# A state-space mixer with its gate's product read from PSUM, its norm in six calls, and one product moved from GpSimd to ScalarE

## The chip, the cores and the metric

The kernel runs on one core of a Trainium2 chip. A core has five engines that run side by side, each through its own list of instructions in order: TensorE (PE, the matrix products; its weight loads are listed apart as PEld), VectorE (DVE), ScalarE (ACT), GpSimd (POOL) and SyncE (SP, here a queue of DMAs). They meet in semaphores only. The on-chip memory is SBUF; matrix products land in PSUM, of which there are eight banks. The metric is the device time of one execution in microseconds (us).

## The reference

A trunk of two layers over 1040 tokens (16 learned ones ahead of 1024) of 1024 features: layer 0 is a Mamba-2 state-space mixer (SSD) and a gated FFN with a convolution, layer 1 a stick-breaking attention and the same kind of FFN. The change is in the mixer alone:

```python
z, xbc, dt_raw = split(u @ w_in)                 # 2048 + 3072 + 32 columns
xbc = silu(causal_dwconv(xbc, conv_w, conv_b))   # 4 taps
xs, b_in, c_in = split(xbc)                      # 2048 | 4 groups x 128 | 4 x 128
dt = softplus(dt_raw + dt_bias); xdt = xs * dt
a_cs = cumsum(dt * -exp(a_log))                  # within a chunk
y_diag = (c_in . b_in) * exp(a_cs[l] - a_cs[s]) @ xdt       # s <= l
chunk_states = b_in^T @ (exp(a_cs[-1] - a_cs) * xdt)
y = y_diag + exp(a_cs) * c_in @ state + d_skip * xs
hg = y * silu(z)                                  # per group of 512 columns:
hg = hg * rsqrt(mean(hg * hg) + eps) * gate_g
out = hg @ w_out
```

## The kernel before

Features lie on partitions, tokens along the row. Each fp32 product is made of three of rounded parts (`mm3`, L150 to L155: high by high, high by low, low by high), so a projection of one block of 128 columns over one of three token tiles (348, 348 and 344 tokens, `TT`) is 24 matmuls into one PSUM bank `pj`. The mixer (from L637 on) first projects group 0's six blocks (four of `x`, one of `b`, one of `c`), and then runs a loop of four groups by nine chunks of 116 tokens. A chunk is `ssd_front`, some projection tiles, and `ssd_back`. The tiles come from one stream, numbered n here: the blocks into group 1, gate of group 0, into group 2, gate of 1, into 3, gate of 2, gate of 3; 18 tiles go by during group 0, 30 during each of groups 1 and 2, 18 during group 3 (two a chunk in groups 0 and 3, three or four in 1 and 2), 6 are left over. Inside this loop the lists of PE, DVE, ACT and POOL are in the order in which the code is written; SP's DMAs are put in order by a scheduler.

- A tile of an `into` block: 24 matmuls (PE), the convolution's first tap by ACT (L275) and three more by DVE (L278), a silu by ACT (L459) that is issued with the next tile.
- A tile of a gate block: 24 matmuls, silu from the bank into an SBUF buffer `z` by ACT (L491), product with the group's `y` rows in place by DVE (L498), square by ACT (L503), sum over the group's four blocks by DVE (L507, L509). In group 3 the product waits until its chunk is done.
- The norm of a gate group, one call for each token tile (`gate_norm`, L515): `rstd` sums the squares over partitions by a matmul into a bank `ms` (L186), takes Ln and Exp on ACT (L189, L190) with a table load ahead of them (L177), refines by four DVE operations (L191 to L194, the second of which reads `ms`), and then four DVE operations scale the rows (L520). The calls stand ahead of tiles n = 31, 32, 33 (61, 62, 63 and 91, 92, 93). Behind the third of groups 0 and 1 the rows are sent to DRAM by four POOL DMAs (`spill`, L357, `y_d`), and their SBUF buffers go to later `xbc` blocks.
- `ssd_front`: on PE c·b (`cb`), the four transposes `px` of x, and the transpose `pb` of b; on DVE the masked `cbm`, `xdt` = px · dt (L597), and the decay matrix times `cbm` (L598); on ACT the copy `bk` of `pb` (L604); on POOL `xde` = xdt · decay to the chunk's end (L606).
- `ssd_decays` of the next chunk is issued in three parts behind the tiles: DMA loads of D and E; eight DVE subtractions (L573) and an Exp on ACT (L574); E times c on POOL (L577).
- `ssd_back`: the state's matmul `S` = bk · xde (L619), the state's update (POOL L625, DVE L626), 16 matmuls `y` (L631, L633) and four DVE operations that add them to the rows (L635).

PSUM in this loop: the projection turns over three banks; `cb`, `pb`, `ms` and `y` over three (pool `sm`); `px` and `S` over two.

## Time and profile before

| | |
|---|---|
| median of the runs | 3048.41 us (3046.30 to 3048.53) |
| the profiled execution | 3046.06 us, its span 3044.3 |
| PE, PEld busy | 95%, 91% of the span |
| DVE, ACT, POOL busy | 76%, 54%, 43% |
| granted TensorE clock, mean | 0.979 |

The four-group loop runs from about 150 to about 740 us; everything ahead and behind keeps its order. Rows give engine, line, operation, out<-in without buffer numbers, partitions x elements; a line number is one of the kernel before unless said. In the timeline `[2.58 <-DVE z L192]` means that the engine stood idle for 2.58 us ahead of that instruction and what released it.

### The profile page before, as it was taken

Reading aid. Unit: us, or ns where it says so; the run is one execution under the profiler, and the core shown is the slowest. Engines: PE = TensorE matmul, PEld = TensorE weight load, DVE = VectorE, ACT = ScalarE, POOL = GpSimd, SP = SyncE. Lnnn points to the kernel's source line nnn. Section 1 sums busy time; section 2 is a strip of 40 time slices with the busy share of each in tenths; the row PEclk is TensorE's granted clock in tenths of the full one; section 3 lists DMA queues with packets and bytes.
Section 4 is the critical chain, followed back from the end, with each engine's and each line's share of the span. In section 5 each row is a group of like instructions: output and inputs, shape, how many; then the busy total and the mean of one; then the engine's idle time right before and its main releaser. Section 6 shows DMA issues by size and latency. Waiting matters only on the chain. (4 is left out here: it accounts for less than half of the span.)

```text
span 3044.3 us, 58681 instructions
## 1 busy us (share of the span) xinstructions
PE 2887.7 (95%) x22535; PEld 2771.6 (91%) x22535; DVE 2312.5 (76%) x4062; ACT 1650.1 (54%) x3403; POOL 1310.2 (43%) x1257
## 2 busy tenths in 40 slices
PE   5999999989997999999999999999898999999997
PEld 2999898979997999998999999999797999999996
DVE  3686868885459877888876888888759888778874
ACT  3555555553245565555334888887636555655332
POOL 1154434452225766663343222222335666663441
PEclk8999999999998999999999999999998999999998
DMA  3333333323121222225232222221431222225231
GB/s 115 106 94 91 109 89 104 103 75 135 61 93 56 75 80 84 77 88 186 64 127 80 59 65 64 68 61 50 141 106 64 84 78 74 81 85 189 77 99 56
DMA packets 123221, 273.42 MB, mean 90 GB/s; under 512 B 13468, under 2 KB 53020, under 8 KB 122940
## 3 DMA queue, kind: packets, MB, share of 16 engines
q1 hardware_dynamic: 117622, 258.54, 27.3%
q10 hardware_dynamic: 4054, 6.56, 0.6%
q8 instruction: 177, 2.90, 0.4%
q0 software_dynamic: 1264, 4.57, 0.4%
q14 instruction: 104, 0.85, 0.1%
HBM read 201.25 MB, written 53.45 MB: 84 GB/s over the span
## 5 line engine op out<-in xcount | busy, mean ns | idle before, releaser
L153 PE MATMUL pj<-uh,wh 128*128 128x348 f32 (+2 forms) x1536 | 506.3, 330 | 9.5 <-ACT bk L604 6.4
L154 PE MATMUL pj<-ul,wh 128*128 128x348 f32 (+2 forms) x1536 | 497.7, 324 | 0.0
L155 PE MATMUL pj<-uh,wl 128*128 128x348 f32 (+2 forms) x1536 | 495.7, 323 | 0.7 <-POOL wl L1150 0.7
L154 PE MATMUL p<-bl,fh 128*128 128x262 f32 x1408 | 401.2, 285 | 14.0 <-DVE bl L814 14.0
L153 PE MATMUL p<-bh,fh 128*128 128x262 f32 x1408 | 402.1, 286 | 1.6 <-ACT fh L845 1.1
L155 PE MATMUL p<-bh,fl 128*128 128x262 f32 x1408 | 400.2, 285 | 0.0
L846 POOL TENSOR_TENSOR fl<-x,fh 128x1024 fp32r<-128x1024 f32 x88 | 212.5, 2415 | 363.2 <-ACT fh L845 277.4
L147 POOL TENSOR_TENSOR wl<-w,wh 128x1024 fp32r<-128x1024 f32 (+2 forms) x80 | 165.4, 2070 | 351.0 <-ACT wh L146 351.0
L154 PE MATMUL p<-bl,wh 128*128 128x262 f32 x1056 | 303.5, 288 | 8.6 <-DVE bl L814 8.6
L153 PE MATMUL p<-bh,wh 128*128 128x262 f32 x1056 | 302.2, 287 | 6.2 <-ACT bh L813 6.2
L153 PEld LDWEIGHTS pj<-uh,wh 128*128 128x128 f32 x1536 | 292.0, 190 | 15.5 <-ACT bk L604 6.9
L155 PE MATMUL p<-bh,wl 128*128 128x262 f32 x1056 | 302.2, 286 | 0.0
L154 PEld LDWEIGHTS pj<-ul,wh 128*128 128x128 f32 x1536 | 292.2, 190 | 1.2 <-issue 0.5
L155 PEld LDWEIGHTS pj<-uh,wl 128*128 128x128 f32 x1536 | 291.6, 190 | 1.1 <-POOL wl L1150 1.0
L278 DVE SCALAR_TENSOR_TENSOR c<-p,params,c 128x260 f32<-128x260 f32 x528 | 251.7, 484 | 51.8 <-ACT c L275 41.9
L154 PEld LDWEIGHTS p<-bl,fh 128*128 128x128 f32 x1408 | 266.9, 190 | 16.2 <-DVE bl L814 16.1
L153 PEld LDWEIGHTS p<-bh,fh 128*128 128x128 f32 x1408 | 267.1, 190 | 3.9 <-ACT fh L845 1.5
L154 PE MATMUL acc<-gl,wh 128*128 128x260 f32 x896 | 255.3, 286 | 13.3 <-DVE gl L995 13.3
L155 PEld LDWEIGHTS p<-bh,fl 128*128 128x128 f32 x1408 | 266.8, 190 | 0.1
L153 PE MATMUL acc<-gh,wh 128*128 128x260 f32 x896 | 251.5, 285 | 7.9 <-DVE p L1040 7.7
L155 PE MATMUL acc<-gh,wl 128*128 128x260 f32 x896 | 254.1, 286 | 0.0
L886 DVE TENSOR_TENSOR c<-c,c 128x260 f32<-128x260 f32 x176 | 248.7, 1414 | 4.2 <-ACT c L882 1.4
(311 smaller groups left out, 8429.7 us busy)
## 6 DMA issues: line engine op xcount, KB each, us to landing
w<-in_w_up SPq DMA_DIRECT2D x88, 512.0 KB
g<-c SPq DMA_DIRECT2D x176, 130.0 KB
w<-in_w_down SPq DMA_DIRECT2D x44, 512.0 KB
w<-in_w_in SPq DMA_DIRECT2D x40, 512.0 KB
b<-g SPq DMA_DIRECT2D x32, 520.0 KB
E<-ea_d SPq DMA_DIRECT2D x32, 464.0 KB
D<-acs_d SPq DMA_DIRECT2D x32, 420.5 KB
h<-h_d SPq DMA_DIRECT2D x16, 520.0 KB
```

The lines of the kernel that those rows point to most:

```text
L147: nc.gpsimd.tensor_tensor(wl[:, :n], w32[:, :n], wh[:, :n].bitcast(F32), op=ALU.subtract)
L153: mm(out, wh, uh, start=first, stop=False, skip_group_check=joins)
L154: mm(out, wh, ul, start=False, stop=False, skip_group_check=joins)
L155: mm(out, wl, uh, start=False, stop=last, skip_group_check=joins)
L278: nc.vector.scalar_tensor_tensor(out, ps[:, o + i : o + i + n], wcol(i), out, op0=ALU.mult, op1=ALU.add)
L846: tt(lo[:, :n], t, hi[:, :n].bitcast(F32), op=ALU.subtract)
L886: self.last_up = tt(g[:, :FN], g[:, :FN], v[:, :FN], op=ALU.mult)
```

## The change

- `xde` is made by ACT instead of POOL: eight operations of 116x64 (one a head, with that head's scale per partition) straight from `px`, issued behind the chunk's first tile (`end`, line 617 of the kernel after). The columns `dte` take in `dt` for that, by one more DVE product at the start. POOL loses 32 operations, ACT gains 256.
- `pb` and its copy `bk` are issued at the front of `ssd_front`, ahead of `cb`.
- `rstd` gets `early`: ACT copies `ms` into an SBUF buffer between Ln and Exp (L193 of the kernel after), and the DVE operation reads the copy. In all 12 norm calls the bank is so left by ACT.
- The norm is issued in six calls: n = 31, 33, 35 the `rstd` of one token tile, n = 32, 34, 36 its four scalings. The spill stands behind n = 36 instead of 33.
- In gate groups 0 to 2 (36 of 48 tiles) the silu is written back into the bank `pj`, and DVE's product reads it there; the square goes to a buffer of its own.

```diff
@@ rstd
-    def rstd(self, accs, n, width, y=None, table=True):
+    def rstd(self, accs, n, width, y=None, table=True, early=False):
-        ps = self.sm("ms")
+        ps = bank = self.sm("ms")
...
         nc.scalar.activation(y, ps[:, :n], AF.Ln, scale=1.0 / width)
+        if early:
+            ps = self.tmp("ms")
+            nc.scalar.activation(ps[:, :n], bank[:, :n], AF.Copy)
         nc.scalar.activation(y, y, AF.Exp, scale=-0.5)
         nc.vector.tensor_tensor(b[:, :n], y, y, op=ALU.mult)
         nc.vector.tensor_tensor(b[:, :n], b[:, :n], ps[:, :n], op=ALU.mult)
@@ dt_path
         nc.scalar.activation(dte, dte, AF.Exp)
+        tt(dte, dte, dt, op=ALU.mult)
@@ gate_group
-                z = self.tmp("z")
+                z = ps if now else self.tmp("z")
                 nc.scalar.activation(z[:, :n], ps[:, :n], AF.Silu)
...
                 tt(xq, xq, z[:, :n], op=ALU.mult)
+                z = self.tmp("z") if now else z
@@ gate_norm
-    def gate_norm(self, g, x, acc, j):
+    def gate_norm(self, g, x, j, r):
         s0, n = TT[j]
-        r = self.rstd([acc.pop(j)], n, DI // GROUPS)
@@ stream
-                for j in range(3):
+                for j in range(6):
                     calls[3 * len(todo) + 1 + j] = lambda f=f, j=j: f(j)
@@ ssd_front
+        bk = None
+        if c < 8:
+            pb = self.sm("pb")
+            nc.tensor.transpose(pb[:n, :P], bt[:, t0:e], self.ident)
+            bk = pool.tile([P, P], F32, tag="bk", name=self.nm("bk"), bufs=2)
+            nc.scalar.activation(bk[:n], pb[:n, :P], AF.Copy)
         pcb = self.sm("cb")
...
-            nc.gpsimd.tensor_tensor(xde[:n], xdt[:n], self.cols[:n, 2, cc, h0 : h0 + GH].unsqueeze(2).to_broadcast([n, GH, 64]), op=ALU.mult)
-        return xdt, xde, bk
+
+        def end():
+
+            xde = pool.tile([P, GH, 64], F32, tag="xde", name=self.nm("xde"), bufs=2)
+            for i in range(GH):
+                nc.scalar.activation(xde[:n, i], px[:, i], AF.Copy, scale=self.cols[:n, 2, cc, h0 + i : h0 + i + 1])
+            return xde
+
+        return xdt, end, bk
@@ mixer
-                def norm(j):
-                    self.gate_norm(g, rows[g], accs[g], j)
-                    if j == 2 and g < 2:
+                r = {}
+
+                def norm(i):
+                    j = i // 2
+                    if i % 2 == 0:
+                        r[j] = self.rstd([accs[g].pop(j)], TT[j][1], DI // GROUPS, early=True)
+                    else:
+                        self.gate_norm(g, rows[g], j, r.pop(j))
+                    if i == 5 and g < 2:
...
-                return self.gate_group(u, g, rows[g], accs[g], later if g == 3 else lambda j, f: f()) + [(None, norm)]
+                return self.gate_group(u, g, rows[g], accs[g], later if g == 3 else lambda j, f: f(), g < 3) + [(None, norm)]
...
                             if given == (tiles * c + 8) // 9:
+                                xdt, end, bk = ops
+                                ops = xdt, end() if c < 8 else None, bk
```

Three places of the lists show it. First ACT in a two-tile chunk of group 0, from the chunk's first convolution tile on. Before:

```order
134 L275 ACTIVATE xbc_1352<-pj_1437,params 128x348 [waits PE_49]
135 L459 ACT_TABLE_LOAD
136 L459 ACTIVATE xbc_1352<-xbc_1352 128x348
137 L275 ACTIVATE xbc_1352<-pj_1471,params 128x344 [waits PE_49]
138 L459 ACTIVATE xbc_1352<-xbc_1352 128x348 [waits DVE_49]
139 L574 ACT_TABLE_LOAD [waits DMAHW1_49]
```

and after:

```order
137 L279 ACTIVATE xbc_1367<-pj_1450,params 128x348 [waits PE_49]
138 L465 ACT_TABLE_LOAD
139 L465 ACTIVATE xbc_1367<-xbc_1367 128x348
140 L617 ACTIVATE xde_1480<-px_1440,cols 116x64 [waits DVE_49,Activation_49]
141 L617 ACTIVATE xde_1480<-px_1440,cols 116x64 x7
142 L279 ACTIVATE xbc_1367<-pj_1493,params 128x344 [waits PE_49]
143 L465 ACTIVATE xbc_1367<-xbc_1367 128x348 [waits DVE_49]
```

Between the first tile's silu and the second tile's convolution now stand the eight products, the first of which waits for DVE and for an earlier ACT operation.

Second PE at the front of chunk 5 of group 1, up to the first matmul of tile n = 35. Before:

```order
1741 L589 MATMUL cb_3132<-xbc_2088,xbc_1929 116x116 [waits DVE_49]
1742 L592 MATMUL px_3134<-ident,xbc_1203 116x128 [waits PE_49]
1743 L592 MATMUL px_3134<-ident,xbc_1352 116x128
1744 L592 MATMUL px_3134<-ident,xbc_1561 116x128
1745 L592 MATMUL px_3134<-ident,xbc_1720 116x128
1746 L602 MATMUL pb_3144<-ident,xbc_1929 116x128 [waits DVE_49]
1747 L153 MATMUL pj_3150<-uh_127,wh_2837 128x348 [waits Activation_49]
```

and after (`ms_3226` is the third token tile's sum of squares of gate group 0, `pb_3209` the transposed b of the same chunk):

```order
1740 L598 MATMUL pb_3209<-ident,xbc_1970 116x128
1741 L602 MATMUL cb_3213<-xbc_2145,xbc_1970 116x116 [waits Activation_49]
1742 L605 MATMUL px_3215<-ident,xbc_1202 116x128 [waits PE_49]
1743 L605 MATMUL px_3215<-ident,xbc_1367 116x128
1744 L605 MATMUL px_3215<-ident,xbc_1581 116x128
1745 L605 MATMUL px_3215<-ident,xbc_1756 116x128
1746 L187 MATMUL ms_3226<-z_2446,ones 128x344 [waits Activation_49]
1747 L153 MATMUL pj_3237<-uh_127,wh_2922 128x348 [waits DVE_49,PE_49]
```

`pb` no longer waits for DVE; the third `ms` has come to this place, directly behind `px`, and waits for an ACT operation: it takes the bank of this chunk's own `pb`, which `bk` (L600) gives back. Before, the third `ms` stood ahead of tile n = 33, behind the 24 matmuls of tile 32 and in another bank than the chunk's `pb`.

Third ACT around the same place: from the D of chunk 5 (`D_3086`) to the convolution of tile n = 36. Before, from the third norm call to there:

```order
260 L574 ACT_TABLE_LOAD [waits DMAHW5_49]
261 L574 ACTIVATE D_3006<-D_3006 116x928 [waits DVE_49]
262 L275 ACTIVATE xbc_3035<-pj_3075,params 128x348 [waits PE_49]
263 L459 ACT_TABLE_LOAD
264 L459 ACTIVATE xbc_3035<-xbc_3035 128x348
265 L604 ACTIVATE bk_3146<-pb_3144 116x128 [waits PE_49]
266 L275 ACTIVATE xbc_3035<-pj_3150,params 128x344 [waits PE_49]
267 L459 ACTIVATE xbc_3035<-xbc_3035 128x348 [waits DVE_49]
268 L146 ACTIVATE wh_3186<-w_420_3184 128x1024 [waits DMAHW7_49,Pool_49]
269 L275 ACTIVATE xbc_3190<-pj_3191,params 128x348 [waits DMASW2_49,PE_49]
```

and after:

```order
283 L581 ACT_TABLE_LOAD [waits DMAHW5_49]
284 L581 ACTIVATE D_3086<-D_3086 116x928 [waits DVE_49]
285 L279 ACTIVATE xbc_3108<-pj_3152,params 128x348 [waits PE_49]
286 L465 ACT_TABLE_LOAD
287 L465 ACTIVATE xbc_3108<-xbc_3108 128x348
288 L600 ACTIVATE bk_3211<-pb_3209 116x128 [waits PE_49]
289 L177 ACT_TABLE_LOAD
290 L190 ACTIVATE y_3228<-ms_3226 128x344 [waits PE_49]
291 L193 ACTIVATE ms_3230<-ms_3226 128x344
292 L194 ACTIVATE y_3228<-y_3228 128x344 [waits Activation_49]
```

and further on in the kernel after, up to the Exp of chunk 6's D:

```order
297 L617 ACTIVATE xde_3267<-px_3215,cols 116x64 x7
298 L146 ACTIVATE wh_3282<-w_423_3280 128x1024 [waits DMAHW7_49,Pool_49]
299 L279 ACTIVATE xbc_3295<-pj_3296,params 128x348 [waits DMASW2_49,DVE_49,PE_49]
300 L465 ACTIVATE xbc_3108<-xbc_3108 128x344
301 L581 ACT_TABLE_LOAD [waits DMAHW1_49]
302 L581 ACTIVATE D_3276<-D_3276 116x928 [waits DVE_49]
```

`bk_3211` still stands behind D's Exp, a convolution and a table load; the third norm's Ln, copy and Exp now follow it. In both kernels the convolution of tile n = 36 writes a buffer that the spill sets free and waits for a DMA (`DMASW2`); the spill is issued three tiles later after the change, right ahead of that tile.

More of the change, by code (lines that the diff above doesn't have):

```diff
@@ L479, in in_group, with gate_group @@
             block(2 * DI + g * P, 16 + g), block(2 * DI + (GROUPS + g) * P, 20 + g)]
-    def gate_group(self, u, g, x, acc, later):
+    def gate_group(self, u, g, x, acc, later, now):
         nc = self.nc
@@ L598, in ssd_front @@
         tt(dk, dk, cbm[:n, :n].unsqueeze(1).to_broadcast([n, GH, n]), op=ALU.mult)
-        bk = xde = None
-        if c < 8:
-            pb = self.sm("pb")
-            nc.tensor.transpose(pb[:n, :P], bt[:, t0:e], self.ident)
-            bk = pool.tile([P, P], F32, tag="bk", name=self.nm("bk"), bufs=2)
-            nc.scalar.activation(bk[:n], pb[:n, :P], AF.Copy)
+        def end():
             xde = pool.tile([P, GH, 64], F32, tag="xde", name=self.nm("xde"), bufs=2)
-            nc.gpsimd.tensor_tensor(xde[:n], xdt[:n], self.cols[:n, 2, cc, h0 : h0 + GH].unsqueeze(2).to_broadcast([n, GH, 64]), op=ALU.mult)
-        return xdt, xde, bk
+            for i in range(GH):
+                nc.scalar.activation(xde[:n, i], px[:, i], AF.Copy, scale=self.cols[:n, 2, cc, h0 + i : h0 + i + 1])
+            return xde
+        return xdt, end, bk
     def ssd_back(self, g, x, c, dk, ce, xdt, xde, bk, state, pool):
```

## Prediction

> **What bounds the kernel now.** I read the busy shares first, then stretches of the loop, the list of waits in them, and the timeline where the waits lie. PE is busy 95% of the span and the chain that ended last is its; so the question is how much PE time the loop loses. Stretches (us; PE, PEld, DVE, ACT, POOL busy; granted clock; DMA):
>
> ```profile
> 150.00:270.00 120.00, 120.00 (x914) 112.36 (x914) 94.17 (x216) 67.58 (x92) 59.74 (x32) 1.00 0.33 97
> 270.00:400.00 130.00, 123.65 (x878) 114.81 (x877) 100.50 (x199) 66.67 (x98) 57.66 (x33) 0.96 0.33 95
> 400.00:550.00 150.00, 143.72 (x1016) 135.15 (x1015) 113.29 (x228) 76.68 (x113) 62.61 (x35) 0.98 0.34 98
> 550.00:700.00 150.00, 137.37 (x1041) 125.94 (x1041) 125.02 (x239) 80.01 (x118) 71.80 (x37) 0.98 0.28 84
> ```
>
> In the first (group 0) PE never stands still. In groups 1 and 2 (second and third) it stands 6.35 + 6.28 = 12.6 us and loses 0.04·130 + 0.02·150 = 8.2 to the clock: 20.8. In group 3 it stands 12.6 and loses 0.02·150 = 3.0: 15.6. The whole change can win 36 us at most. What it waits for, from 150 to 740 us (total, times, longest):
>
> ```profile
> PE pb L602 <- DVE z L192: 6.8, 3, 2.6
> PE ms L186 <- ACT bk L604: 6.6, 3, 5.8
> PE S L619 <- POOL xde L606: 3.6, 4, 1.1
> PE y L631 <- DVE D L598: 1.5, 1, 1.5
> ACT D L574 <- DVE D L573: 107.6, 35, 7.8
> ```
>
> and where it does in groups 1 and 3:
>
> ```profile
> 325.07 0.33 PE L602 MATMUL pb<-ident,xbc 128*116 128x128 f32 x1 [2.58 <-DVE z L192]
> 355.20 0.63 PE L153 MATMUL pj<-uh,wh 128*128 128x352 f32 x1 [3.22 <-ACT bk L604]
> 355.63 0.49 PE L154 MATMUL pj<-ul,wh 128*128 128x352 f32 x1
> 355.93 0.49 PE L155 MATMUL pj<-uh,wl 128*128 128x352 f32 x1
> ...
> 361.35 0.32 PE L153 MATMUL pj<-uh,wh 128*128 128x352 f32 x1
> 361.51 0.32 PE L154 MATMUL pj<-ul,wh 128*128 128x352 f32 x1
> ...
> 654.75 0.32 PE L602 MATMUL pb<-ident,xbc 128*116 128x128 f32 x1 [1.74 <-DVE z L192]
> 660.90 1.53 PE L186 MATMUL ms<-z,ones 128*128 128x348 f32 x2 [5.82 <-ACT bk L604]
> ```
>
> The long waits of PE, all but those for `xde` and D, lie at a norm or right behind one. After one, matmuls start every 0.30 us (355.63, 355.93) instead of 0.16 (361.35, 361.51): the slow clock.
>
> **The change, part by part.**
>
> *Norm in six calls, bank left at once, b first (groups 1, 2).* The waits of `pb` for DVE go: ACT's copy now frees `ms`. The first two `ms` of a group have banks that were freed long before, and the wait of `pj`, whose convolution stood late behind three norms, goes with the heap. That would free all 20.8. But the third `ms` now stands directly behind `px` of chunk 5 and takes the bank of that chunk's `pb`, so PE waits for `bk`, which ACT does behind D's Exp, which waits for DVE. Before, that `bk` came 11 us behind its `pb`. Durations (PE, ACT; DVE and what held it; then a chunk of group 0 on ACT and PE):
>
> ```profile
> 343.60 0.27 PE L602 MATMUL pb<-ident,xbc 128*116 128x128 f32 x1
> 354.92 0.26 ACT L604 ACTIVATE bk<-pb 116x128 f32<-116x128 f32 x1
> ...
> 341.98 0.51 DVE L191 TENSOR_TENSOR z<-y 128x344 f32<-128x344 f32 x1
> ...
> 343.44 0.52 DVE L194 TENSOR_TENSOR y<-y,z 128x344 f32<-128x344 f32 x1
> 345.94 1.81 DVE L278 SCALAR_TENSOR_TENSOR xbc<-pj,params,xbc 128x348 f32<-128x348 f32 x3
> 658.07 1.60 DVE L573 TENSOR_SCALAR D<-D,cols 116x116 f32<-116x116 f32 x8
> 351.70 0.98 ACT L574 ACTIVATE D<-D 116x928 f32<-116x928 f32 x1 [7.82 <-DVE D L573]
> ...
> 335.57 2.69 DVE L194 TENSOR_TENSOR y<-y,z 128x348 f32<-128x348 f32 x1
> 335.49 2.39 POOL L147 TENSOR_TENSOR wl<-w,wh 128x1024 fp32r<-128x1024 f32 x1 [1.26 <-ACT wh L146]
> ...
> L189 ACT ACTIVATE y<-ms 128x348 f32<-128x348 f32 (+1 forms) x12 | 5.5, 460 | 0.6 <-PE ms L186 0.5
> ...
> 204.10 0.64 ACT L275 ACTIVATE xbc<-pj,params 128x344 f32<-128x344 f32 x1 [1.98 <-PE pj L155]
> 204.76 1.28 ACT L459 ACT_TABLE_LOAD   x1
> 206.05 0.50 ACT L459 ACTIVATE xbc<-xbc 128x348 f32<-128x348 f32 x1
> 206.46 1.04 ACT L146 ACTIVATE wh<-w 128x1024 fp32r<-128x1024 f32 x1
> 207.73 1.02 PE L619 MATMUL S<-xde,bk 116*128 116x512 f32 x2
> ...
> 210.49 0.46 PE L589 MATMUL cb<-xbc,xbc 128*116 128x116 f32 x2
> 211.25 0.41 PE L153 MATMUL pj<-uh,wh 128*128 128x352 f32 x1
> ```
>
> I count from the end of tile n = 32 on PE. PE: two tiles of 24 · 0.16 = 3.84 each, state and `y` matmuls 2.76 (207.73 to 210.49), the front 0.76 (to 211.25), the second `ms` (two more matmuls) 0.3: ready for the third at 11.5. ACT: convolution 0.64, silu 0.5, eight `xde` products 1.6 (below), weight copy 1.04, table 1.28, Ln 0.46, the copy of `ms` and Exp as much again each: 6.4, less some overlap at the starts, 6.2. DVE from there: the norm's four 1.98 (341.98 to 343.96), convolution 1.81, eight subtractions 1.60: 11.6. ACT again: D's Exp 0.98, convolution 0.64, table 1.28, silu 0.5, `bk` 0.26: 15.3. So PE waits 3.8 if nothing holds DVE. The row at 335.57 shows what may: an operation that took 0.52 at 343.44 took 2.69 beside POOL's 2.39; with one such, 6.0. A POOL operation is about as likely there as not (it is busy in 44% and 42% of these stretches): I take 5.0, and the clock loss that such waits had. Groups 1 and 2 had four waits of over 2 us, so 8.2/4 = 2.05 each. That makes 7.05 a group; ends 3.8 (no slow clock) and 8.1.
>
> *The spill three tiles later.* The convolution of n = 36 writes a buffer that the spill frees. Before, its issue lay about 11.6 us (three tiles) earlier:
>
> ```profile
> DMA to landing us min/median/max: 7.9/9.0/10.2
> ```
>
> Now it is issued behind the third call's first scaling, in the same place of ACT's list as that convolution. Tile 36 itself runs 3.84 on PE, so of a landing 7.9 to 10.2 after issue ACT stands about 4 to 6 us there, and D's Exp of chunk 6, its `bk` and the next convolutions stand behind it. PE has two more tiles in free banks, 7.7 us, and a chunk's end and front, 3.5. I take 2.0 of wait (nearer to none, by that cover) and 0.5 of clock; ends 0 and 6, if the subtractions behind the convolution are held too. Groups 1 and 2 so lose 2 · (7.05 + 2.5) = 19.1 for 20.8: **−1.7**.
>
> *xde on ACT.* POOL's 59.1 us go:
>
> ```profile
> L606 POOL TENSOR_TENSOR xde<-xdt,cols 116x512 f32<-116x512 f32 x32 | 59.1, 1847 | 198.8 <-DVE xdt L597 186.1 <-DMA E<-ea_d 12.7
> 1690.84 0.40 ACT L1261 ACTIVATE kp<-lg,rt 116x116 f32<-116x116 f32 x1
> 1691.08 0.41 ACT L1262 ACTIVATE bt<-lg,rt 116x116 f32<-116x116 f32 x1
> ```
>
> An ACT operation from a bank with a scale per partition starts every 0.24 us at 116x116; for 116x64 I take 0.2, so eight are 1.6 and the last ends 0.2 later. In group 0 the chain is the convolution of a chunk's first tile at 204.10, table, silu (to 206.46), xde to 208.3, where `S` started at 207.73 without a wait: 0.6 late, in seven chunks (the first has no table load on that path): **+4**; ends 0 (0.1 a piece) and 6.3 (0.24). Waits this short I cost without a clock loss. In groups 1 and 2 two or three tiles lie behind it. In group 3 no table load stands between a gate silu and `xde`, which so ends 208.3 − 1.28 = 207.0, 0.7 us ahead of `S`: the four waits for POOL, 3.6 us, go.
>
> *Products from PSUM.*
>
> ```profile
> L498 DVE TENSOR_TENSOR xbc<-xbc,z 128x348 f32<-128x348 f32 (+1 forms) x48 | 56.7, 1184 | 14.8 <-ACT z L491 14.8
> L597 DVE TENSOR_TENSOR xdt<-px,cols 116x512 f32<-116x512 f32 (+1 forms) x36 | 24.4, 679 | 0.2 <-PE px L592 0.2
> ```
>
> The product from SBUF takes 0.52 alone and 1184 ns in the mean, because POOL holds it; `xdt`, which reads PSUM, 679 with 512 columns. 36 products save up to 36 · 0.66 = 24 us of DVE off the path, and the bank then waits for DVE instead of ACT, under two tiles' cover (7.7 us). The longer hold, one product of about 0.52, falls inside it: 0; if that cover is gone, 12 tiles a group at 0.52, 6 us each. The Trainium skill, SBUF — State Buffer, section Who interferes with whom, says that a DVE instruction with two SBUF inputs contends with a GpSimd instruction that reads SBUF, and one of the two fully blocks; the rows here (335.57 beside 335.49) agree. That rule speaks against the copy of `ms`: an operation that read PSUM now has two SBUF inputs. By the rule the wait of the third `ms` would go by its end 6.0, 2 · 1.0 us more in the sum: 3040.7.
>
> *Group 3.* Its `pb` wait (1.74) and `ms` wait (5.82) go, since all three `ms` there stand in the middle of a chunk and `pb` is first; with them 3.0 of clock and 3.6 of xde, and about 1.5 at small ones: 15.6 less what I leave, the `y` wait for D (1.5) and as much again of the clock and new bank waits: **−12**; ends −6 and −14.
>
> *The rest.* Twelve copies of `ms` on ACT, 0.4 each, and 24 xde of groups 1 to 3, 1.8 each, lie in ACT's own wait for D (107.6 us); without that cover they would cost 4.8 + 43 us, under 2 a chunk. The product dte · dt is one DVE operation of 288 columns, under 0.52: 0. The orders ahead of and behind the loop are unchanged.
>
> Sum: −1.7 + 4 − 12 = −9.7 on the profiled execution's 3046.06 (span 3044.3), so 3036.4. The median of the runs, 3048.41, is 2.35 above that execution: **3038.7**. What a measurement can tell from no change is about 0.2%, 6.1 us.
>
> **Rivals.**
> 1. *The third `ms` costs nothing* (DVE, rid of blocked products, has D ready early): for it speaks that 3.8 is a small difference of two chains of 11 to 15 us; against, that `bk` lay 11.3 us behind `pb` there before (343.60 to 354.92) with the third norm's work not yet behind it. Groups 1, 2 then lose 2 · 2.5: −15.8 + 4 − 12 = −23.8, 3024.6.
> 2. *The group 3 waits stay*, the copy of `ms` standing behind other ACT work as `bk` did: of the 15.6 only the `xde` waits go, −12 becomes −4, total −1.7: 3046.7, no change. Against: `ms` does not stand behind `px` there.
> 3. *Slower: the spill.* ACT stands at n = 36 until the landing. From the scaling it is 9.0 to landing, then 0.64 and 1.81 of convolution, 11.45 in all, before that bank is free and DVE may go on to chunk 6's subtractions; 1.6 and 0.98 more to the D that `y` needs. If PE's cover is only tile 36, since it is already late from the third `ms` and the banks are held by products and convolutions that wait on the same ACT list, it loses 11.45 − 3.84 + 1.6 + 0.98 = 10.2 and 2.05 of clock a group for 2.5: 2 · 9.75 = 19.5 more, +9.8, 3058.2. It is slower by what can be told from 2 · 7.9 more on, a loss of 10.4 a group there. For it speaks that every step of ACT behind that convolution is needed by chunk 6; against, that `y` of chunk 6 lies 15 us of PE work away (four tiles).
>
> **How the numbers follow.** Forecast 0.60 (its own range 3031 to 3047: the ends of the third `ms`, the spill, `xde` and group 3, not all on one side), rival 1 0.12, rival 2 0.13, rival 3 0.15. Faster: 0.45 of the first, all of rival 1, 0.02 of rival 2: 0.59. Same: 0.13 + 0.09 + 0.03 = 0.25. Slower: 0.16. For 8 in 10 the range reaches to rivals 1 and 3: 3024 to 3056.
>
> **What will show it.** Right: no wait of `pb`, none of `S` for POOL, `ms` of n = 35 and 65 waiting 3.8 to 6 us behind `px` for ACT, `S` of group 0 waiting about 0.6 in seven chunks, PE idle from 550 to 700 under 4. Wrong: those `ms` waits absent; ACT's convolution of n = 36 followed by PE waits over 5 us; a clock under 0.98 in group 0, which would mean that its short waits do cost clock.

## The result and the profile after

The changed kernel took 3048.76 us in the median (3046.59 to 3050.85), the kernel before, beside it, 3046.76 (3043.46 to 3048.53); the ratio is 1.0007, 95% interval 0.9999 to 1.0016. The forecast was a gain of 9.7 us; there is none that can be told from zero. The profiled execution took 3047.72, with a span of 3046.0.

The loop itself can be read more closely than the whole: it runs from the first `cb` on PE to the first matmul `acc` behind it, and each group from its first `cb` to the next group's. From those starts in the timelines:

| us | group 0 | group 1 | group 2 | group 3 | loop |
|---|---|---|---|---|---|
| before | 103.56 | 158.22 | 157.01 | 138.80 | 557.59 |
| after | 109.21 | 160.43 | 159.01 | 127.53 | 556.18 |
| measured difference | +5.65 | +2.21 | +2.00 | −11.27 | −1.41 |
| forecast | +4 | −0.85 | −0.85 | −12 | −9.7 |

Outside the loop the two profiled executions differ by 3.1 us the other way (1.7 of span and 1.4 of loop), where the orders of the instructions are the same; that is the size by which executions differ.

Stretches of the loop after the change (us; PE, PEld, DVE, ACT, POOL busy; granted clock; DMA):

```profile
150.00:270.00 120.00, 115.92 (x878) 106.24 (x877) 97.45 (x209) 75.96 (x158) 44.26 (x23) 1.00 0.31 94
270.00:400.00 130.00, 119.84 (x847) 111.82 (x846) 82.11 (x190) 76.48 (x147) 42.43 (x25) 0.96 0.32 94
400.00:550.00 150.00, 139.92 (x1005) 130.51 (x1006) 98.97 (x224) 88.76 (x174) 50.50 (x28) 0.98 0.31 95
550.00:700.00 150.00, 145.83 (x1130) 134.99 (x1127) 124.56 (x262) 103.30 (x204) 59.93 (x30) 1.00 0.31 91
```

Group 0, where PE never stood, now stands 4.1 us; groups 1 and 2 stand 10.2 and 10.1 where they stood 6.35 and 6.28, at the same mean clocks; group 3 stands 4.2 instead of 12.6, at full clock. POOL has less to do everywhere and ACT more; DVE has less in the last three stretches and 3 us more in the first (97.45, before 94.17).

Groups 1 and 2 so stand 7.6 us more and are only 4.2 longer. The mean clock hides why: half of the slow stretch at each `ms` now falls in the wait itself. In group 1 the clock is 0.50 from 348.40 to 351.80, while PE stands, and from 351.80 to 355.20, while it works. PE works at half clock for three stretches of 3.4 us in the two groups (behind each `ms`, and behind the wait at 375.58), a loss of 5.1 us. The waits from 150 to 745 us (total, times, longest):

```profile
PE ms L187 <- ACT bk L600: 14.5, 2, 7.3
PE S L632 <- ACT xde L617: 6.3, 10, 1.3
PE pj L153 <- DVE xbc L282: 4.9, 4, 2.4
ACT xbc L279 <- DMA y_d<-xbc: 18.3, 2, 9.8
ACT D L581 <- DVE D L580: 82.0, 35, 4.7
```

No `pb` waits any more. In their place stand two waits of `ms`, and ACT stands for the landing of the spill. On PE's timeline (two chunks of group 0; then group 1's chunk 5 and tile n = 37):

```profile
187.84 1.13 PE L632 MATMUL S<-xde,bk 116*128 116x512 f32 x2 [1.22 <-ACT xde L617]
211.52 1.12 PE L632 MATMUL S<-xde,bk 116*128 116x512 f32 x2 [0.34 <-ACT xde L617]
...
351.80 1.52 PE L187 MATMUL ms<-z,ones 128*128 128x344 f32 x2 [7.26 <-ACT bk L600]
...
375.58 0.54 PE L153 MATMUL pj<-uh,wh 128*128 128x352 f32 x1 [2.40 <-DVE xbc L282]
```

Why `ms` waits 7.26, from DVE, POOL and ACT ahead of it:

```profile
335.06 1.75 ACT L617 ACTIVATE xde<-px,cols 116x64 f32<-116x64 f32 x8 [1.33 <-DVE xdt L610]
...
340.30 2.49 DVE L195 TENSOR_TENSOR z<-y 128x348 f32<-128x348 f32 x1 [0.56 <-ACT y L194]
342.83 1.25 DVE L196 TENSOR_TENSOR z<-z,ms 128x348 f32<-128x348 f32 x1
...
346.64 1.59 DVE L580 TENSOR_SCALAR D<-D,cols 116x116 f32<-116x116 f32 x8
337.84 2.45 POOL L147 TENSOR_TENSOR wl<-w,wh 128x1024 fp32r<-128x1024 f32 x1 [8.20 <-ACT wh L146]
340.25 2.17 POOL L584 TENSOR_TENSOR E<-E,xbc 128x928 f32<-128x928 f32 x1
342.37 1.32 POOL L638 TENSOR_TENSOR state<-state,cd 128x512 f32<-128x512 f32 x1
...
348.27 0.98 ACT L581 ACTIVATE D<-D 116x928 f32<-116x928 f32 x1 [4.37 <-DVE D L580]
...
351.49 0.26 ACT L600 ACTIVATE bk<-pb 116x128 f32<-116x128 f32 x1
```

ACT's `xde` of chunk 4, ahead of the second norm, stands 1.33 us for DVE's `xdt`. The second norm's first DVE operation takes 2.49 instead of 0.51 beside POOL's E (340.25), and its second, which reads the copy of `ms`, 1.25 instead of 0.51 beside POOL's state product (342.37). D's subtractions so end at 348.2, D's Exp runs to 349.2, and `bk`, behind a convolution, a table load and a silu, ends at 351.75. The `ms` of the third token tile starts at 351.80.

And the spill:

```profile
360.49 2.03 DVE L527 SCALAR_TENSOR_TENSOR xbc<-xbc,params,y 128x344 f32<-128x344 f32 x4
362.02 1.11 ACT L146 ACTIVATE wh<-w 128x1024 fp32r<-128x1024 f32 x1
363.21 2.38 POOL L147 TENSOR_TENSOR wl<-w,wh 128x1024 fp32r<-128x1024 f32 x1 [19.51 <-ACT wh L146]
365.53 2.19 POOL L361 DMA_DIRECT2D y_d<-xbc  x4
372.95 0.64 ACT L279 ACTIVATE xbc<-pj,params 128x348 f32<-128x348 f32 x1 [9.82 <-DMA y_d<-xbc]
```

The scalings begin at 360.49 and the first is through at 361.0. The DMAs are issued at 365.53 only: POOL's list has the weight product `wl` ahead of them, which waits for ACT's `wh`, and that stands behind the eight `xde`. ACT stands 9.82 us for the landing.

### The profile page after: what moved, and what is told of

Same layout as the page of the kernel before. It is cut to its first block, busy times and chain, and to the rows that moved or that the text cites. A ratio compares the mean times of both kernels' runs of the same rounds, so it can differ in the third digit from the quotient of the medians.

```text
span 3046.0 us, 58945 instructions
## 1 busy us (share of the span) xinstructions
PE 2885.6 (95%) x22535; PEld 2768.2 (91%) x22535; DVE 2285.9 (75%) x4063; ACT 1705.9 (56%) x3672; POOL 1254.8 (41%) x1225
## 5 line engine op out<-in xcount | busy, mean ns | idle before, releaser
L154 PE MATMUL acc<-gl,wh 128*128 128x260 f32 x896 | 255.8, 287 | 12.6 <-DVE gl L1016 12.6
```

The source lines that it names most:

```text
L154: mm(out, wh, ul, start=False, stop=False, skip_group_check=joins)
```

## The experiments

Two questions: is it the place of the third `ms` and of the spill that takes groups 1 and 2, and the place of `xde` that takes group 0? "The changed kernel" is the one whose result stands above. Lines are those of each kernel's own file.

### 1. The third rstd one tile earlier

```diff
-                    calls[3 * len(todo) + 1 + j] = lambda f=f, j=j: f(j)
+                    calls[3 * len(todo) + (1 + j if len(todo) > 20 else (1, 2, 3, 5, 4, 6)[j])] = lambda f=f, j=j: f(j)
```

> One edit to the changed kernel: in groups 1 and 2 the third rstd call is issued ahead of tile n = 34 (64) instead of 35 (65), so its ms stands in the middle of chunk 4 and takes a bank that was freed long before; the second call's scalings go to n = 35, the spill stays at n = 36. Theory (the third ms gives the gain of groups 1 and 2 back): the two waits of ms for bk, 7.26 and 7.21 us, go, and with them about 2 us of slow clock each; waits for the spill's buffer stay at 2 to 4 us a group. Total 14 to 18 us under the changed kernel, about 3031 to 3035. Rival (the wait only moves: PE comes 7 us earlier to the convolution of n = 36 that waits for the spill, and waits there instead): waits of pj behind n = 36 grow to 6 to 9 us a group, total 0 to 6 us under the changed kernel.

Measured: 3047.53 us, ratio 1.0008 (0.9999 to 1.0018); loop 558.35. The waits of `ms` went, and nothing was won: PE waited nearly as long at `cb` of chunk 5 (6.94 and 6.90 in the two groups). PE and ACT:

```profile
351.60 0.73 PE L602 MATMUL cb<-xbc,xbc 128*116 128x116 f32 x2 [6.94 <-ACT ms L193]
...
348.45 0.98 ACT L581 ACTIVATE D<-D 116x928 f32<-116x928 f32 x1 [4.38 <-DVE D L580]
...
351.10 0.45 ACT L193 ACTIVATE ms<-ms 128x344 f32<-128x344 f32 x1
```

The third `ms` now had a free bank, but its copy stood behind D's Exp on ACT (351.10 behind 348.45), and `cb` wanted that bank. The theory was too narrow, and the rival had the wrong place for the right thought: the wait moved to the next bank that ACT frees behind D's Exp, not to the spill.

### 2. xde at the front of the chunk

```diff
                         now = dk, ce
+                        xdt, end, bk = ops
+                        ops = xdt, end() if c < 8 else None, bk
...
-                                xdt, end, bk = ops
-                                ops = xdt, end() if c < 8 else None, bk
```

> One edit to the changed kernel: the eight xde operations on ACT stand directly behind bk, ahead of the chunk's first tile, instead of behind that tile's convolution, table load and silu. Theory (the xde waits give part of the gain back, by their place behind the silu and not by their length): the seven waits of S in group 0 (4.07 us in all) and the three in group 3 (2.2) go; group 0, which took 109.2 us instead of 103.6, comes back to 103.5 to 104.5; total 5 to 8 us under the changed kernel. Rival (ACT has no room: eight more operations ahead of the convolution make the next tiles' banks late): group 0 stays above 107 us with waits of pj in place of those of S, total within 2 us of the changed kernel.

Measured: 3073.18 us, ratio 1.0091 (1.0076 to 1.0106), 24 us above the changed kernel; every group is longer or as long (108.6, 164.6, 165.6, 141.9). ACT in a chunk of group 0, and its waits in the loop:

```profile
221.27 0.26 ACT L600 ACTIVATE bk<-pb 116x128 f32<-116x128 f32 x1
222.81 1.75 ACT L617 ACTIVATE xde<-px,cols 116x64 f32<-116x64 f32 x8 [1.28 <-DVE xdt L610]
...
ACT xde L617 <- DVE xdt L610: 75.7, 30, 6.2
```

`xde` reads the same bank as DVE's `xdt` and waits until that is through: ACT stands 1.28 us in this chunk and 75.7 in the loop, and everything behind it is late. The Trainium skill, PSUM — Partial Sum Buffer, section PSUM bank collisions raise a hardware error, says that two engines may not touch the same partitions of one bank at once, and that the compiler puts a dependency between them, for reads too. The wait here is in line with that; neither theory had it. The place behind a tile, where the change put `xde`, hides most of it: there ACT stands 17.4 us for `xdt` in the loop.

### 3. The product from SBUF

```diff
-                return self.gate_group(u, g, rows[g], accs[g], later if g == 3 else lambda j, f: f(), g < 3) + [(None, norm)]
+                return self.gate_group(u, g, rows[g], accs[g], later if g == 3 else lambda j, f: f(), False) + [(None, norm)]
```

> One edit to the changed kernel: the silu of gate groups 0 to 2 goes to an SBUF buffer again and the product reads it there, as in the kernel before. Theory (the product's source saves DVE time off the path and is worth little): DVE busy rises by 10 to 24 us in the loop, the time stays within 3 us of the changed kernel, the third ms's wait stays at 6 to 9 us. Rival (DVE is what D's Exp and so bk wait for, and the product is in that chain): the waits of groups 1 and 2 grow by over 5 us, total 5 to 12 us above the changed kernel.

Measured: 3055.09 us, ratio 1.0026 (1.0017 to 1.0036); loop 561.28, 5.1 above the changed kernel: 0.8, 1.1 and 3.3 in groups 1, 2 and 3. The waits of `ms` grew by 0.5 each (7.71, 7.70). The interval is just clear of the changed kernel's (0.9999 to 1.0016). The time lies in the rival's range, but not for the rival's reason: PE's waits in groups 1 and 2 grew by 1.3 us together, not by over 5. Of the 3.3 us in group 3, where the product had not been counted at all, about half is clock: a wait of `S` was followed by 3.4 us at a clock of 0.50 (652.70 to 656.10), and the changed kernel has no such stretch there. Such a stretch also comes and goes in kernels whose edits leave group 3 alone: without it the group takes 127.5 (changed kernel) and 128.3 (run 7), with it 129.9 to 130.3 (runs 1, 9 and 12). Set beside its like, this run's 130.8 is 0.5 to 0.9 us longer, and run 10's 129.8, which has no such stretch, 1.5 to 2.3. So in these profiles the product from PSUM is worth 1 to 2 us in groups 1 and 2 together (run 10 and this one) and some 0.5 to 2 in group 3. DVE's product of the changed kernel and of this one:

```profile
L505 DVE TENSOR_TENSOR xbc<-xbc,pj 128x348 f32<-128x348 f32 (+1 forms) x36 | 18.2, 508 | 19.4 <-ACT pj L498 19.4
```
```profile
L505 DVE TENSOR_TENSOR xbc<-xbc,z 128x348 f32<-128x348 f32 (+1 forms) x48 | 52.7, 1102 | 14.8 <-ACT z L498 14.8
```

### 4. xde on POOL again

```diff
-            for i in range(GH):
-                nc.scalar.activation(xde[:n, i], px[:, i], AF.Copy, scale=self.cols[:n, 2, cc, h0 + i : h0 + i + 1])
+            nc.gpsimd.tensor_tensor(xde[:n], xdt[:n], self.cols[:n, 2, cc, h0 : h0 + GH].unsqueeze(2).to_broadcast([n, GH, 64]), op=ALU.mult)
```

It is issued at the front of the chunk, and the product of the columns with dt goes.

> One part undone in the changed kernel: xde is made by POOL from xdt again, at the front of the chunk, and the columns are not multiplied by dt. Theory: group 0 goes back to about 103.6 us (5.6 less), the four waits of S for POOL in group 3 come back (3.6 in place of 2.2), ACT's chain ahead of the third ms is 1.6 us shorter but DVE is held by POOL more often, so that the waits of ms stay at 5 to 9 us: total 2 to 6 us under the changed kernel. Rival (POOL's xde holds DVE's chain wherever the norm stands, and its leaving was what freed group 3): group 3, 127.5 us in the changed kernel, goes back above 133, total 0 to 6 us above the changed kernel.

Measured: 3052.02 us, ratio 1.0017 (1.0007 to 1.0026); loop 558.95. That is not told apart from the changed kernel (0.9999 to 1.0016), and not the 2 to 6 us of gain that the theory had. Group 0 came back to 103.3, as said. Group 3 stayed at 129.9, against the rival, and of the four waits of `S` for POOL one came back (1.62). But the third `ms` waited 10.9 us in both groups, over what the theory gave it (5 to 9). PE, then DVE and POOL ahead of it in this kernel, and the same scalings on DVE in the changed kernel:

```profile
348.20 1.51 PE L187 MATMUL ms<-z,ones 128*128 128x344 f32 x2 [10.88 <-ACT bk L599]
...
330.12 7.66 DVE L526 SCALAR_TENSOR_TENSOR xbc<-xbc,params,y 128x348 f32<-128x348 f32 x4
331.06 2.67 POOL L147 TENSOR_TENSOR wl<-w,wh 128x1024 fp32r<-128x1024 f32 x1
```
```profile
335.98 2.05 DVE L527 SCALAR_TENSOR_TENSOR xbc<-xbc,params,y 128x348 f32<-128x348 f32 x4
```

The four scalings ahead of D's subtractions take 7.66 us beside POOL, which has `xde`, `wl` and E to do there from 329.25 to 336.13; in the changed kernel they take 2.05, with POOL idle beside them. So `xde` on ACT costs 5.9 us in group 0 (109.2 for 103.3) and saves 3.6 us at each of those two waits, because POOL holds DVE less there.

### 5. The norm in three calls again

```diff
-                    calls[3 * len(todo) + 1 + j] = lambda f=f, j=j: f(j)
+                    k = 3 * len(todo) + 1 + j // 2
+                    calls[k] = lambda f=f, j=j, first=calls.get(k, lambda: None): (first(), f(j))
```

> One part undone in the changed kernel: the norm is issued in three calls again (each rstd with its scalings, ahead of n = 31, 32, 33, and the spill behind n = 33); the copy of ms, the early b, the product from PSUM and xde on ACT stay. Theory (a bank that ACT frees behind D's Exp is what PE waits for, so an ms next to a chunk's front waits for the bk of that chunk): the third ms, now in the middle of chunk 4, waits for nothing; the second, which comes to stand directly behind px of chunk 4, waits for that chunk's bk, 2 to 6 us; the spill is issued early enough that the convolution of n = 36 does not wait for its landing. Groups 1 and 2 together 6 to 12 us under those of the changed kernel (160.4 and 159.0). Rival (the six calls are not what costs): groups 1 and 2 within 3 us of it.

Measured: 3050.74 us, ratio 1.0016 (1.0007 to 1.0025). Groups 1 and 2 took 155.4 and 154.3, 9.7 us less than the changed kernel's: as the theory had it, though the second `ms` waited 0.6 instead of 2 to 6, and PE stood 3.2 us at a projection for chunk 5's `bk`. Group 3 took 139.6 instead of 127.5, with the wait of `ms` that the kernel before had (5.82) and a longer one of `y` (before 1.50):

```profile
658.76 1.53 PE L187 MATMUL ms<-z,ones 128*128 128x348 f32 x2 [5.24 <-ACT bk L601]
684.04 0.75 PE L645 MATMUL y<-D,xdt 112*64 112x112 f32 x4 [3.68 <-DVE D L612]
```

Six calls, at the places that the change gave them, free group 3 and cost groups 1 and 2. The two nearly cancel: in the whole the run is not told apart from the changed kernel.

### 6. xde ahead of the silu

```diff
                         now = dk, ce
+                        xdt, end, bk = ops
+                        xde = []
+                        if c < 8:
+                            self.open.insert(0, lambda end=end, xde=xde: xde.append(end()))
...
-                                xdt, end, bk = ops
-                                ops = xdt, end() if c < 8 else None, bk
...
-                        state = self.ssd_back(g, x, c, *now, *ops, state, pool)
+                        state = self.ssd_back(g, x, c, *now, xdt, xde[0] if c < 8 else None, bk, state, pool)
```

> One edit to the changed kernel: the eight xde operations stand directly behind the convolution's first tap of the chunk's first tile, ahead of the table load and silu that follow it (in a gate tile behind its silu). DVE's xdt, for which they wait, is done by then. Theory (group 0 lost its time to the 1.8 us of table load and silu ahead of xde): the waits of S in group 0 and 3 go, group 0 comes to 103.3 to 104.5 us from 109.2, the rest stays: total 5 to 8 us under the changed kernel. Rival (more work ahead of the silu delays whoever waits for ACT, as with xde at the front): group 0 over 107 us, or groups 1 and 2 longer by over 4 us: no gain.

Measured: 3051.51 us, ratio 1.0016 (1.0006 to 1.0025). Group 0 took 105.7: five of its seven waits went and two of 0.87 stayed. Groups 1 and 2 became 1.3 and 3.5 us longer: the third `ms` waited still longer for `bk`, 8.92 and 8.95. Each theory held in its own place, and the sum is no gain.

### 7. Both later rstd calls ahead of D's Exp, the spill a tile earlier

```diff
-                    calls[3 * len(todo) + 1 + j] = lambda f=f, j=j: f(j)
+                    k = 3 * len(todo) + (1 + j if len(todo) > 20 else (1, 2, 3, 4, 3, 5)[j])
+                    calls[k] = lambda f=f, j=j, first=calls.get(k, lambda: None): (first(), f(j))
```

> One edit to the changed kernel: in groups 1 and 2 the second and the third rstd are both issued ahead of n = 33 (63), ahead of chunk 5's D in ACT's list; the scalings at n = 32, 34 and 35, the spill behind n = 35. Both copies of ms then stand ahead of D's Exp. Theory (what PE waits for is a bank that ACT frees behind D's Exp): neither the third ms nor cb of chunk 5 waits over 1 us, the spill's landing is waited for by less than 4 us on ACT and by nothing on PE: groups 1 and 2 together 14 to 20 us under the changed kernel's 319.4, total about 3028 to 3034. Rival (the wait moves on to the next bank: DVE has two norm chains ahead of D's subtractions, so D's Exp and all behind it come later by 2 to 4 us): waits of over 3 us at pj or cb in chunks 5 or 6, gain under 8 us.

Measured: 3030.53 us, ratio 0.9948 (0.9934 to 0.9961), 18.2 below the changed kernel. Groups 1 and 2 took 150.67 and 150.57, together 18.2 less. ACT and POOL at chunk 5 and n = 36:

```profile
342.92 0.45 ACT L193 ACTIVATE ms<-ms 128x344 f32<-128x344 f32 x1
...
351.19 0.98 ACT L582 ACTIVATE D<-D 116x928 f32<-116x928 f32 x1 [3.81 <-DVE D L581]
...
363.40 0.64 ACT L279 ACTIVATE xbc<-pj,params 128x348 f32<-128x348 f32 x1 [3.47 <-DMA y_d<-xbc]
359.02 2.18 POOL L361 DMA_DIRECT2D y_d<-xbc  x4 [14.32 <-DVE xbc L527]
361.22 2.39 POOL L147 TENSOR_TENSOR wl<-w,wh 128x1024 fp32r<-128x1024 f32 x1
```

The third copy (342.92) stands 8 us ahead of D's Exp (351.19), the spill ahead of `wl`, and ACT waits 3.47 for the landing instead of 9.82. No wait of PE in the two groups is over 1.2 us; PE stands 3.3 and 3.2 us where it stood 10.2 and 10.1, and the granted clock in them is 1.00 instead of 0.97 and 0.98. That is the theory as run 1 had mended it: PE must not want a bank that ACT gives back behind D's Exp.

### 8. Runs 6 and 7 together

Its edit is that of runs 6 and 7.

> The two edits together: both later rstd calls ahead of n = 33 (63), spill behind n = 35, and xde directly behind the first tap. Theory: their gains add, 20 to 28 us under the changed kernel, about 3020 to 3028, clear of the kernel before. Rival: one of them does not hold, and the sum is that of the other alone, 3 to 10 us under the changed kernel, no different from before or up to 0.3% faster.

Measured: 3035.49 us, ratio 0.996 (0.9948 to 0.9973): 5 us above run 7, though the two intervals overlap; loop 542.97, 4.3 more. The gains do not add, and the result is that of neither expectation. Group 0 won its 3.5 (105.7), groups 1 and 2 lost 2.9 and 2.8, group 3 2.1. As in run 6, `xde` ahead of the silu costs elsewhere what it saves in group 0; the 2.1 of group 3 alone would not show it (see run 12).

### 9. Run 7 with the spill at n = 36

```diff
-(1, 2, 3, 4, 3, 5)[j]
+(1, 2, 3, 4, 3, 6)[j]
```

> The kernel with both later rstd calls ahead of n = 33, but the third call's scalings and the spill at n = 36, as in the changed kernel. It tells the two parts of that edit apart. Theory (the spill's place is a second, smaller cost: its issue stands behind POOL's wl, which waits for ACT's weight copy): ACT stands 8 to 11 us for the landing, PE waits 2 to 4 us more a group: 4 to 9 us above that kernel. Rival (without the third ms's wait the landing is hidden): within 2 us of it.

Measured: 3040.10 us, ratio 0.998 (0.9971 to 0.9989), 9.6 above run 7; groups 1 and 2 took 155.28 and 155.12, 4.6 each more. POOL and PE:

```profile
359.48 2.64 POOL L147 TENSOR_TENSOR wl<-w,wh 128x1024 fp32r<-128x1024 f32 x1 [15.31 <-ACT wh L146]
362.07 2.32 POOL L361 DMA_DIRECT2D y_d<-xbc  x4
...
370.59 0.63 PE L153 MATMUL pj<-uh,wh 128*128 128x352 f32 x1 [4.42 <-DVE xbc L282]
```

The spill is behind `wl` again, ACT stands 8.6 us, and PE 4.42. Of the 4.6 us a group half to two thirds is standing (5.51 and 6.16 us, in run 7 3.29 and 3.19) and the rest the clock, 0.98 and 0.99 instead of 1.00. So run 7's 18 us are half the place of the `ms` (160.43 + 159.01 to 155.28 + 155.12: 9.0) and half that of the spill (9.2). In the changed kernel the spill's wait looked smaller (2.40 and 0.50), and there PE had already stood at `ms`.

### 10. Run 7 with the product from SBUF

The edit is that of run 3, made in run 7's kernel.

> The kernel with both later rstd calls ahead of n = 33, but the gate product of groups 0 to 2 from an SBUF buffer. Theory (the product from PSUM takes DVE time away from where D's Exp waits for it; worth 5 us of loop in the changed kernel, most of it in group 3): 3 to 8 us above that kernel. Rival (with the third ms's wait gone DVE has room): within 2 us of it.

Measured: 3033.40 us, ratio 0.9952 (0.9939 to 0.9966); loop 541.26 for 538.71, +2.6: 0.6 and 0.5 in groups 1 and 2, 1.55 in group 3, between the two theories. In the median 2.9 us show, which the intervals don't tell apart from run 7. The loop loses 2.5 us less than in run 3; 1.7 of that is the slow stretch in group 3 that run 3 had and this run has not (clock 1.00), so it is not shown that DVE's time is worth less here.

### 11. Run 7 without the copy of ms

```diff
-                        r[j] = self.rstd([accs[g].pop(j)], TT[j][1], DI // GROUPS, early=True)
+                        r[j] = self.rstd([accs[g].pop(j)], TT[j][1], DI // GROUPS)
```

> The kernel with both later rstd calls ahead of n = 33, but without ACT's copy of ms: DVE's second operation reads the bank and frees it. Theory (the calls in the middle of a chunk leave DVE 11 us until the next chunk's pb and cb want those banks): groups 1 and 2 within 2 us each, group 3 longer by the pb wait it had before (1.7 and its clock): 0 to 5 us above that kernel. Rival (the bank left at once is what freed PE, as the change means it): waits of pb or cb for DVE of over 2 us in groups 1 and 2, 8 to 14 us above that kernel.

Measured: 3027.55 us, ratio 0.9931 (0.9915 to 0.9946); loop 536.15, 2.6 under run 7. The bank left at once was not needed here, and the copy cost a little in the loop; the whole times of the two are not told apart. The norm's second DVE operation with and without it:

```profile
L196 DVE TENSOR_TENSOR z<-z,ms 128x348 f32<-128x348 f32 (+1 forms) x12 | 10.9, 909 | 0.3
```
```profile
L196 DVE TENSOR_TENSOR z<-z,ms 128x348 f32<-128x348 f32 (+1 forms) x12 | 6.2, 513 | 0.3
```

Reading the copy it takes 909 ns in the mean, reading the bank 513. In run 7 the seven of the twelve with POOL idle beside them take 0.50 to 0.52 us; the five that begin 0.45 us behind the start of a POOL operation take 1.24 to 2.33. In this run all twelve take 0.50 to 0.52, five of them just so beside POOL. The Trainium skill, SBUF — State Buffer, section Who interferes with whom, says that a DVE instruction with two SBUF inputs contends with a GpSimd instruction that reads SBUF; these rows agree. Group 3, where a `pb` wait of 1.7 was expected back, took 127.8.

### 12. Run 7 with xde on POOL in group 0

```diff
+        if g == 0 and c < 8:
+            early = pool.tile([P, GH, 64], F32, tag="xde", name=self.nm("xde"), bufs=2)
+            nc.gpsimd.tensor_tensor(early[:n], xdt[:n], self.cols[:n, 3, cc, h0 : h0 + GH].unsqueeze(2).to_broadcast([n, GH, 64]), op=ALU.mult)
         return xdt, end, bk
```

Column 3 holds the decay without dt, and `end` gives `early` back in group 0.

> To the kernel with both later rstd calls ahead of n = 33 one edit more: in group 0 xde is made by POOL from xdt at the chunk's front, as before the change; groups 1 to 3 keep it on ACT. Theory: group 0 goes from 109.2 to about 103.4 us and nothing else moves: about 3024 to 3026, ratio to before 0.992 to 0.994. Rival (POOL's xde holds DVE operations that the faster loop needs): group 0 stays over 106, gain under 3 us.

Measured: 3029.55 us, ratio 0.9939 (0.9927 to 0.9952). Group 0 took 103.29, the loop 534.88, 3.8 under run 7; group 3, which the edit does not touch, was 2.1 longer (130.33). Its waits of `S` sum to 3.3 us instead of 2.1, and its last long wait is as long as in run 7, but is followed by a slow stretch here and not there. This run, then run 7:

```profile
662.21 0.44 PE L650 MATMUL y<-D,xdt 112*64 112x112 f32 x3 [2.09 <-issue]
```
```profile
667.13 0.44 PE L645 MATMUL y<-D,xdt 112*64 112x112 f32 x3 [2.07 <-issue]
```

The clock is 0.50 from 663.10 to 666.50 in this run, a loss of 1.7 us, and 1.00 behind 667.13 in run 7. Runs 1 and 9, whose edits leave group 3 alone as well, have it at 129.9 and 130.3 with a clock of 0.99. So a difference of 2 to 3 us in group 3 between two single profiles shows nothing by itself. In the median only 1.0 us shows against run 7's 3030.53, which the intervals don't tell apart. Runs 7, 11 and 12 are all clear of both kernels, not of one another; 11 and 12 together were not run.

## Why the prediction was right or wrong

The time lay inside the range of 3024 to 3056, and the case of no change had 0.25; the likeliest case, 9.7 us faster, was wrong. That the range held is owed to its width: no change came mainly by two waits that were longer than forecast, not by rival 2, the case that forecast it. By its steps:

- *Norm in six calls, the third `ms`: wrong in size.* The mechanism was there as forecast, behind `px` of chunk 5, for `bk`, in both groups, and with a slow stretch behind it. But the term was taken as 5.0 us of wait and measured 7.26 and 7.21, above its end of 6.0. The count took one DVE operation held by POOL as even odds; two were held (2.49 and 1.25, where 1.98 was counted for all four), the second because of the copy of `ms` (run 11). Against the 3.8 with nothing held these are 2.7 us. ACT's 1.33 us for `xdt` (1.27 in the other group), ahead of the second norm, is in no term; with it the chain comes to 7.8, a little over the wait. The end of 6.0, with one operation held, was nearer than 5.0 and still short.
- *The spill three tiles later: wrong in size, and one queue was left out.* 2.0 us of wait was taken, 2.90 and 2.87 measured (2.40 + 0.50; 1.06 + 0.82 + 0.99). The count had the issue right behind the scaling; in POOL's list `wl` stood ahead of it, 4.5 us. Rival 3's place was right, and its price too high: 9.2 us for both groups by run 9, not 19.5. Together with the `ms` the waits are 2 · (2.2 + 0.9) = 6.2 us over the forecast, and groups 1 and 2 missed it by 5.9 (−1.7 to +4.2). The clock was not missed: 2 · (2.05 + 0.5) = 5.1 us of loss were left in the sum, and 5.1 were measured.
- *xde on ACT in group 0: right in kind, 1.65 us too small.* Seven waits of 0.6 were forecast, 4.2 in all; there were five of 0.30 to 0.34 and two of 1.22, 4.07 in all. In the two chunks of 1.22 the first convolution stands behind D's Exp and `bk` on ACT and so starts late (183.70, behind an Exp at 182.66); the count had it wait for PE only. The group became 5.65 longer, not 4: the wait that the timeline lists runs from the modelled end of the last `pj` matmul, which overlaps its successor when there is one. The start of `S` lies 0.66 behind the start of that matmul instead of 0.15, 0.51 later for a listed 0.34; 0.17 more in each of seven chunks is 1.2; the last 0.4 us stays open. Before, and after:

```profile
207.58 0.32 PE L155 MATMUL pj<-uh,wl 128*128 128x352 f32 x1
207.73 1.02 PE L619 MATMUL S<-xde,bk 116*128 116x512 f32 x2
```
```profile
210.86 0.32 PE L155 MATMUL pj<-uh,wl 128*128 128x352 f32 x1
211.52 1.12 PE L632 MATMUL S<-xde,bk 116*128 116x512 f32 x2 [0.34 <-ACT xde L617]
```

- *Products from PSUM: costed at nothing, worth a few us.* Run 3 lost 5.1 us of loop without them and run 10 2.6; in groups 1 and 2 that is 1.9 and 1.1 together. In group 3, where it lies inside the −12, a slow stretch of 1.7 us that run 3 had is part of it.
- *Group 3: right, and nearer than it could know.* −12 forecast, −11.3 measured; the waits of `pb` and `ms` went, and run 5 brings that of `ms` back with three calls. Its `xde` term was not as forecast: the waits for POOL went, but `S` now waits 1.25 and 0.79 us for ACT, where the sum had none. In runs 1, 9 and 12, which leave group 3 alone, it took 129.9 to 130.3, which would be −8.9 to −8.5; so the last 2 to 3 us of the agreement are luck.
- *Rival 1* (the third `ms` costs nothing) is refuted; *rival 2* (group 3's waits stay) too.
- *The signs.* No wait of `pb` and none of `S` for POOL is left, and group 0 kept its clock of 1.00, as said; the `ms` waits lie above 3.8 to 6, and PE's idle time from 550 to 700 is 4.2, where under 4 was said.
- *The sum.* The loop moved by −1.4 for −9.7: 5.9 of the 8.3 us between lie in groups 1 and 2, 1.65 in group 0, 0.7 in group 3.

## What to carry to other kernels

A bank is free when the engine that empties it gets there, and that engine's list, with what stands ahead, sets the time: the whole cost here hung on whether a copy stood ahead of an Exp that waits for DVE. Moving a call by one tile is not enough if the next bank hangs on the same place; both calls had to go ahead of it. A DMA issue that is moved must be read in the list of the engine that issues it: here three tiles of delay became more than four by a product that stood ahead. When a step gains in one group and loses in another, undo it where it loses; run 7 keeps group 3's gain and beats both kernels. A saving of 2 us in one stretch of one profile may be no more than a slow stretch of the clock that did not come.

## What was not expected of the hardware

- Two reads of one PSUM bank by two engines do not run side by side in this program, the second waits for the first: `xde` on ACT stood 75.7 us in the loop for DVE's `xdt` where it came directly behind it (run 2). By the code `xde` reads nothing that `xdt` writes.
- Eight ACT operations of 116x64 with a scale per partition took 1.73 us, 0.2 apart, as estimated; what they cost came from where they stand.
- DVE's product of 128x348 took 508 ns in the mean with one input from PSUM and 1102 with both from SBUF, with nearly the same POOL work beside it (52.5 and 53.4 us of POOL in group 1; run 3).
- Two waits of PE of the same length need not have the same clock behind them: 2.09 us were followed by 3.4 us at 0.50 (run 12), 2.07 us by none (run 7).
